# Statistics by positions, factors from PSUM, weights by quarters and differences by product in the opening of a hybrid decoder block

## The chip, the core and the metric

The kernel runs on one core of one Trainium2 chip. The metric is device microseconds for one execution, the median of several runs. TensorE (PE) multiplies 128x128 weights with 128x512 operands into PSUM, which has eight banks of 128x512 fp32; VectorE (DVE), ScalarE (ACT) and GpSimd (POOL) do the elementwise work, and SyncE (SP) issues all DMAs of this kernel, on one queue.

## The reference

One layer of a decoder block over 2048 positions of width 1024, in fp32. What matters here is its opening; the rest is named only.

```python
def rmsnorm(x, g):
    y = x * rsqrt(mean(x * x, axis=-1) + 1e-6)
    return y * g

h = rmsnorm(x, norm1_g)           # x: 2048 positions x 1024
proj = h @ w_in                   # 1024 x 3088
# split into q, k, v, g, a (gated linear attention) and b, c, h (short convolution)
# then: attention in chunks, convolution, output projection, residual,
# second rmsnorm, SwiGLU FFN of width 2816, residual, last rmsnorm
```

## The kernel before

**Layout.** Activations are kept with features on partitions and positions on the free axis. The 2048 positions are four blocks of 512 (`PB`), and a feature tile is 128 features; the input comes twice, as `xt` (features on partitions, 256 KB for one tile of one block) and as `x` (positions on partitions). Two blocks make a half; each stage runs for half 0 and then for half 1.

**Products.** Every fp32 matrix is split into a high part `hi` (ScalarE copies it to fp32r, L144) and a remainder `lo` (VectorE subtracts, L145), and a product is three matmuls: weight-hi with operand-hi, weight-hi with operand-lo, weight-lo with operand-hi. A unit (`unit`, matmuls at L321 to L323) does a 2x2 block product with seven products instead of eight (Winograd's form): weights A11, S1, S2, A12, S3, S4, A22 with operands B11, T1, T2, B21, T3, B22, T4. The T's are differences of the scaled input, made on GpSimd: T1 = B12 - B11, T2 = B22 - T1, T3 = B22 - B12, T4 = B21 - T2. The S's come from a 1 MB weight load `raw` of four quarters, also by GpSimd differences (L304 to L311).

**The opening**, which the change touches, is this. `first_stats` loads 16 tiles of `xt`, eight for block 0 and eight for block 1, with the first weights `raw` between them. ScalarE squares each tile (L418, L421), the squares of block 0 are added on VectorE and those of block 1 on GpSimd (L423), and a matmul with a matrix of ones sums over partitions (`column_rstd`, L159); `finish_rstd` makes the factor 1/sqrt(mean + eps), as a 128x512 tile in SBUF, with VectorE and ScalarE operations on the full tile (L165, then L149 to L153). `build_first` then goes through block 0 (`j` = 0) and block 1 (`j` = 1), and in each through eight feature tiles, called columns here: VectorE scales the tile with the norm's weight and factor (`scaled`, L431), ScalarE and VectorE split it into an operand `op` (L144, L145), and TensorE does six matmuls with it (L272 to L274), which give the first unit directly with the four quarters as they are. The VectorE instructions of a column are ordered so that the next tile's scaling stands ahead of the split of this one. The second block's `column_rstd` is issued within the first block (after column 3). After the 16 columns GpSimd makes the differences, column by column: for each of four `k` it does T1, T2, T3, T4 (L281), with one scratch tile `t1` for three of them, and each result is split.

**Order.** A scheduler orders the instructions of each engine by its own timeline; the order on an engine is then fixed, and an instruction waits for all ahead of it. `in_proj` runs twelve units for the half and, between the products of a unit, `tick` steps a queue of background work, in the order `gate_weights`, `gate` (the forget gate's matmuls L488 with `wa_sb`, and scans L516), `row_stats(2)`, `row_stats(3)`, and `h1_ahead`, which makes the operands of half 1.

**What exists already elsewhere.** `row_stats` makes the factors of blocks 2 and 3 from `x` by positions: ScalarE squares a piece with an accumulated sum (L388), VectorE and ScalarE make the factor on a 128x4 tile (L149 to L153), VectorE spreads each of its four columns over a 128x128 tile (L397), and TensorE transposes these into a PSUM bank `rb_ps` (L398), which ScalarE copies to SBUF.

Of the kernel before, what the change touches and what calls it, by code (L numbers as in the profile page):

```python
# [18 lines left out]
P = 128  # L19
D = 1024  # L20
SEQ = 2048
PB = 512
NB = SEQ // PB
KD = D // P
PT = PB // P
# [5 lines left out]
EPS = 1e-6  # L31
# [16 lines left out]
def tile_hymba_block(ctx, tc, x, xt, win, wa, wgu, wout, wffn, wdown, wdown_first, small, out):  # L48
# [7 lines left out]
    opp = pool_of("opp", 28)  # L56
# [139 lines left out]
    def split_op(src):  # L196
        o = opp.tile([P, 2, PB], F32R, name="op", tag="op")
        split(src, o[:, 0, :], o[:, 1, :])
        return o
# [45 lines left out]
            put("B22", k, b22)  # L245
            yield

    def build_first(quad, w, later):


        ops = {b: [] for _, b in PRODUCTS}
        h, o = {}, {}
        quarters = ("A11", "A12"), ("A21", "A22")
        los = []
        for j in range(2):
            for r in range(2):
                o[r, j] = bank()
            for k in range(KD):
                with ExitStack() as stack:
                    if len(los) > 1:  # L260
                        stack.enter_context(tc.issue_after(los[-2].ins))
                    h[k, j] = quad(k, j)
                x = opp.tile([P, 2, PB], F32R, name="op", tag="op")
                los.append(split(h[k, j][:], x[:, 0, :], x[:, 1, :]))
                if (j, k) == (0, 3):
                    rbs[1] = column_rstd(later, D)
                name = ("B11", "B12")[j] if k < 4 else ("B21", "B22")[j]
                ops.setdefault(name, []).append(x)
                c = slice(k % 4 * P, (k % 4 + 1) * P)
                for r in range(2):  # L270
                    q = w[quarters[r][k // 4]]
                    pe.matmul(o[r, j][:], q[:, 0, c], x[:, 0, :], start=k == 0, stop=False)  # L272
                    pe.matmul(o[r, j][:], q[:, 0, c], x[:, 1, :], start=False, stop=False)
                    pe.matmul(o[r, j][:], q[:, 1, c], x[:, 0, :], start=False, stop=k == KD - 1)  # L274
        for k in range(4):
            t1 = bt("t1")
            b11, b12, b21, b22 = h[k, 0], h[k, 1], h[k + 4, 0], h[k + 4, 1]
            for n, y, a, b in (
                ("T1", t1, b12, b11), ("T2", t1, b22, t1), ("T3", b12, b22, b12), ("T4", t1, b21, t1)
            ):  # L280
                pool.tensor_tensor(y[:], a[:], b[:], ALU.subtract)  # L281
                ops[n].append(split_op(y[:]))
        return ops, [(r, j, o[r, j], True) for j in range(2) for r in range(2)]

    def weight_quarter(src):
        n = src.shape[-1]
        h = wqp.tile([P, 2, PB], F32R, name="wq", tag="wq")[:, :, 0:n]
        split(src, h[:, 0, :], h[:, 1, :])
        return h

    def raw_weights(src):
        n = src.shape[-1]
        raw = rawp.tile([P, 4 * PB], F32, name="raw", tag="raw")[:, 0 : 4 * n]
        raw = raw.rearrange("p (a n) -> p a n", a=4)
        raw_loads.append(load(raw, src))
        return raw
# [79 lines left out]
        return s  # L376


    rbs = {}

    def row_stats(b):
        ssq = mtiny.tile([P, PT, 2], F32, name="ssq", tag="ssq")
        for t in range(PT):
            for e in range(2):
                xn = bt("xn")
                r0 = b * PB + t * P
                load(xn[:], x[r0 : r0 + P, e * PB : (e + 1) * PB])
                act.activation(xn[:], xn[:], AF.Square, accum_out=ssq[:, t, e : e + 1])  # L388
            yield
        v, l, y0 = [mtiny.tile([P, PT], F32, name=n, tag=n) for n in ("msq", "rl", "ry")]  # L390
        dve.tensor_tensor(v[:], ssq[:, :, 0], ssq[:, :, 1], ALU.add)
        dve.tensor_scalar(v[:], v[:], 1.0 / D, EPS, ALU.mult, ALU.add)
        rsqrt(v[:], v[:], l[:], y0[:])
        rb_ps = bank("rb_ps")
        for t in range(PT):
            rep = mtiny.tile([P, P], F32, name="rep", tag="rep")
            dve.tensor_copy(rep[:], v[:, t : t + 1].to_broadcast([P, P]))  # L397
            pe.transpose(rb_ps[:, t * P : (t + 1) * P], rep[:], ident[:])  # L398
        rb = bt("rb2")
        act.activation(rb[:], rb_ps[:], AF.Copy)  # L400
        store(s_rb[b][:], rb[:])

    raws, first_weights, last_load = {}, {}, []

    def first_stats():

        for j in range(2):
            for k in range(KD):
                h = bt("h") if j else tt("h")
                raws[j, k] = h  # L410
                last_load[:] = [load(h[:], xt[j, :, k, :])]
            if j == 0:
                raw = raw_weights(win[0])
        ssq = [tiny.tile([P, PB], F32, name="rb2", tag="rb") for _ in range(2)]
        for j in range(2):
            for k in range(KD):
                if k == 0:
                    act.activation(ssq[j][:], raws[j, k][:], AF.Square)  # L418
                else:
                    q = opp.tile([P, 2, PB], F32, name="q", tag="op")  # L420
                    act.activation(q[:, 0, :], raws[j, k][:], AF.Square)  # L421
                    add = pool if j else dve
                    add.tensor_tensor(ssq[j][:], ssq[j][:], q[:, 0, :], ALU.add)  # L423
            if j == 0:
                rbs[0] = column_rstd(ssq[0], D)
                for n, i in (("A11", 0), ("A21", 3), ("A12", 1), ("A22", 2)):
                    first_weights[n] = weight_quarter(raw[:, i, :])
        return ssq[1]

    def scaled(g, rb, h):  # L430
        dve.scalar_tensor_tensor(h[:], h[:], g, rb[:], ALU.mult, ALU.mult)  # L431
# [8 lines left out]
        split(raw[:], w[:, :, 0, :], w[:, :, 1, :])  # L440
        yield

    def build_h(later):


        def quad(k, j):
            return scaled(col(C_G1 + k), rbs[j], raws[j, k])

        return build_first(quad, first_weights, later)

    def h1_ahead():

# [486 lines left out]


    act.preload_act_table_set("natural_log_exp_and_others")
    later = first_stats()
    load(wgu_sb[:], wgu)
    ops, first = build_h(later)
    hurry.append(True)
    background.extend(
        [gate_weights(), gate(0, ops), row_stats(2), row_stats(3), unhurried(), h1_ahead()]
# [124 lines left out]
```

## Time and profile before

| | |
|---|---|
| median of 3 runs | 2182.29 us (2181.57 to 2185.2) |
| profiled execution | 2184.78 us |
| its span in the profile | 2183.0 us |
| granted TensorE clock, mean | 0.982 |
| busy: PE, DVE, ACT, POOL | 2048.8, 1460.2, 996.5, 985.5 us |
| moved by DMA | 467.65 MB |

The span runs from the first to the last instruction of the program; the profiled execution's time has 1.8 us around it. Busy is the time in which an engine executes; TensorE's is 94% of the span over the whole kernel, but not in the first 100 us, where the change is. Starts in the timeline are us from the span's beginning, and a row `x4` merges four instructions of one kind that follow each other; its second number is then the time from the start of the first to the end of the last. Instructions of one engine overlap at their ends, so the pace of a chain is the distance of starts, which is a little less than a duration. A name after `<-` in brackets is what ended the engine's wait.

### The profile page before, as it was taken

To read this page: it belongs to the slowest core of one execution; us is meant where nothing else is said; L and a number is where in the kernel's file an instruction comes from. 1 tells how busy PE (TensorE), PEld (TensorE's weight loads), DVE (VectorE), ACT (ScalarE), POOL (GpSimd) and SP (SyncE) were. 2 spreads that over 40 slices of the span, in tenths; PEclk is the share of its full clock that TensorE was granted. 3 is DMA by queue.
4 is the path that set the end of the run, shared out by engine and by line. 5 is a ranking of instruction groups with operands and counts; after the bars stand their busy time and mean duration, and the time that the engine had idled before them with its cause. 6 is when DMAs were issued, how large, how long until landed. Compare 5 with 4: busy or idle time off the path is not lost.

```text
span 2183.0 us, 26899 instructions
## 1 busy us (share of the span) xinstructions
PE 2048.8 (94%) x9137; PEld 1656.3 (76%) x9137; DVE 1460.2 (67%) x2039; ACT 996.5 (46%) x1940; POOL 985.5 (45%) x706
## 2 busy tenths in 40 slices
PE   4899899999998999999999989998999999989996
PEld 3577677877887887788888868887888888867774
DVE  7859975557763496787877566544666656668755
ACT  4555434564544245455555433333444544434442
POOL 4526431112201273555655456664544445357663
PEclk9999999999999999999999999999999999999998
DMA  4259667532586793466454595698353443598772
GB/s 147 71 202 321 215 246 258 150 111 91 156 289 198 295 309 138 164 234 223 174 227 174 214 357 209 245 347 348 116 183 135 159 160 134 221 361 315 304 266 101
DMA packets 189978, 467.65 MB, mean 214 GB/s; under 512 B 19856, under 2 KB 65168, under 8 KB 180112
## 3 DMA queue, kind: packets, MB, share of 16 engines
q1 hardware_dynamic: 189840, 465.93, 59.2%
q8 instruction: 72, 1.18, 0.2%
q14 instruction: 66, 0.54, 0.1%
HBM read 297.03 MB, written 168.82 MB: 213 GB/s over the span
## 4 chain that ended last, share of the span: by engine, by line
PE 68%; DVE 13%; DMA 9%; ACT 4%; issue 3%; POOL 2%; SPq 1%; DVEq 0%; ACTq 0%; POOLq 0%
PE mm L321 20%; PE mm L323 20%; PE mm L322 20%; DVE wq L145 2%; DVE h L431 2%; DMA op<-shT 1%; DVE op L145 1%; PE mm L709 1%; PE mm L710 1%; PE mm L712 1%; DMA op<-sm 1%; DMA op<-sa_T 1%; DVE c L345 1%; DMA raw<-in_wdown_first_dram 1%; DVE so L145 1%
## 5 line engine op out<-in xcount | busy, mean ns | idle before, releaser
L321 PE MATMUL mm<-op,wq 128*128 128x512 f32 x2495 | 984.2, 396 | 50.9 <-ACT c L341 22.2
L322 PE MATMUL mm<-op,wq 128*128 128x512 f32 x2495 | 977.9, 392 | 4.1 <-DVE op L145 4.1
L323 PE MATMUL mm<-op,wq 128*128 128x512 f32 x2495 | 967.2, 393 | 14.9 <-DVE wq L145 14.5
L145 DVE TENSOR_TENSOR wq<-raw,wq 128x512 fp32r<-128x512 f32 (+2 forms) x628 | 526.6, 845 | 337.8 <-ACT wq L144 335.6
L144 ACT ACTIVATE wq<-raw 128x512 fp32r<-128x512 f32 (+2 forms) x628 | 365.1, 587 | 580.2 <-PE mm L323 408.3
L321 PEld LDWEIGHTS mm<-op,wq 128*128 128x128 f32 x2495 | 471.7, 189 | 167.7 <-ACT c L341 30.7
L323 PEld LDWEIGHTS mm<-op,wq 128*128 128x128 f32 x2495 | 471.6, 189 | 124.7 <-DVE wq L145 24.4
L322 PEld LDWEIGHTS mm<-op,wq 128*128 128x128 f32 x2495 | 472.1, 189 | 102.9 <-DVE op L145 5.1
L306 POOL TENSOR_TENSOR raw<-s,raw 128x512 f32<-128x512 f32 (+2 forms) x98 | 131.5, 1342 | 461.5 <-DVE wq L145 427.2
L345 DVE TENSOR_TENSOR c<-mm,c 128x512 f32<-128x512 f32 x294 | 201.6, 686 | 102.6 <-PE mm L323 97.9
L304 POOL TENSOR_TENSOR s<-raw 128x512 f32<-128x512 f32 (+2 forms) x98 | 130.9, 1336 | 210.8 <-DMA raw<-in_wffn_dram 90.5
L341 ACT ACTIVATE c<-mm 128x512 f32<-128x512 f32 x294 | 170.7, 586 | 31.9 <-PE mm L323 30.8
L311 POOL TENSOR_TENSOR raw<-raw 128x512 f32<-128x512 f32 (+2 forms) x98 | 129.0, 1317 | 119.7 <-DVE wq L145 104.2
L865 POOL TENSOR_TENSOR y<-c,y 128x512 f32<-128x512 f32 x90 | 135.9, 1515 | 92.0 <-DVE c L345 91.8
L691 POOL TENSOR_TENSOR ssx<-ssx,q 128x512 f32<-128x512 f32 x52 | 75.9, 1472 | 144.1 <-ACT q L690 143.6
L305 POOL TENSOR_TENSOR raw<-raw 128x512 f32<-128x512 f32 (+2 forms) x98 | 137.2, 1400 | 4.7
L145 DVE TENSOR_TENSOR so<-t,so 128x512 fp32r<-128x512 f32 x100 | 88.0, 889 | 40.2 <-ACT so L144 39.9
L709 PE MATMUL mm<-op,wq 128*128 128x512 f32 x256 | 101.3, 396 | 0.0
L710 PE MATMUL mm<-op,wq 128*128 128x512 f32 x256 | 100.5, 393 | 0.0
L144 ACT ACTIVATE wq<-s 128x512 fp32r<-128x512 f32 (+2 forms) x98 | 57.5, 587 | 92.0 <-PE mm L323 87.6
L144 ACT ACTIVATE so<-t 128x512 fp32r<-128x512 f32 x100 | 62.7, 629 | 66.5 <-DMA sa_B<-so 35.3
L145 DVE TENSOR_TENSOR wq<-s,wq 128x512 fp32r<-128x512 f32 (+2 forms) x98 | 79.3, 810 | 14.8 <-ACT wq L144 14.2
(170 smaller groups left out, 1856.2 us busy)
## 6 DMA issues: line engine op xcount, KB each, us to landing
raw<-in_wffn_dram SPq DMA_DIRECT2D x44, 1024.0 KB, 5.6
sa_T<-so SPq DMA_DIRECT2D x88, 512.0 KB, 5.0
op<-sa_T SPq DMA_DIRECT2D x88, 512.0 KB, 8.4
sa_B<-so SPq DMA_DIRECT2D x69, 512.0 KB, 3.8
op<-sa_B SPq DMA_DIRECT2D x69, 512.0 KB, 8.6
raw<-in_win_dram SPq DMA_DIRECT2D x24, 1024.0 KB, 5.9
raw<-in_wdown_dram SPq DMA_DIRECT2D x24, 768.0 KB, 6.8
y<-sx SPq DMA_DIRECT2D x64, 256.0 KB, 6.7
```

What stands on the lines that cost most here:

```text
L144: last_hi[:] = [act.activation(hi, src, AF.Copy)]
L145: return dve.tensor_tensor(lo, src, hi.bitcast(F32), ALU.subtract)
L304: pool.tensor_tensor(s1, a21, a22, ALU.add)
L305: pool.tensor_tensor(a21, a11, a21, ALU.subtract)
L306: pool.tensor_tensor(a11, s1, a11, ALU.subtract)
L311: pool.tensor_tensor(a12, a12, a11, ALU.subtract)
L321: pe.matmul(o[:], wh, xh, start=first and k == 0, stop=False, skip_group_check=True)
L322: pe.matmul(o[:], wh, xl, start=False, stop=False, skip_group_check=True)
L323: return pe.matmul(o[:], wl, xh, start=False, stop=k == n - 1, skip_group_check=True)
L341: act.activation(t[:], o[:], AF.Copy)
L345: dve.tensor_tensor(t[:], o[:], t[:], ALU.add)
L865: eng.tensor_tensor(yy, c[:], yy, ALU.add)
```

## The change

1. **Statistics by positions.** The factors of blocks 0 and 1 are made as `row_stats` does it: `first_loads` loads four pieces of `x` for each block (128 positions x 1024, 512 KB each), ScalarE squares each with an accumulated sum (L411), and `rows_rstd` makes the factor on a 128x4 tile, spreads and transposes it. The 14 additions over tiles (L423), the two matmuls with ones and the full-size `finish_rstd` are gone from the opening. The squares of block 1 are issued within block 0's columns 4 to 7 (`row_squares`).
2. **Factors from PSUM.** `rows_rstd` returns the PSUM bank, and `scaled` reads it there (L437); `row_stats` still copies it to SBUF.
3. **Weights by quarters.** The first `raw` is loaded as four DMAs of 256 KB, two ahead of block 0's first four tiles of `xt` and two ahead of its last four. The order of loads is: four of `x`, two quarters, four tiles, two quarters, four tiles, four of `x` for block 1, eight tiles of block 1.
4. **Differences by product.** T1 is made for all four `k`, then T2, T3, T4, each in place in a tile of the scaled input (L283), without the scratch tile.

In the instruction lists as built, the change reaches to TensorE's row 416 of 8869, VectorE's 278 of 2041, ScalarE's 234, GpSimd's 58 and SyncE's 178; the rows after these are the same in both kernels. Within the lists of the changed kernel, GpSimd does T3 ahead of T2, and ScalarE has the splits of the two later weight quarters ahead of the split of the first operand. In the first block TensorE has the four transposes of block 1's factor behind the last matmul of block 0.

```diff
-    def build_first(quad, w, later):
+    def build_first(quad, w):
...
-                if (j, k) == (0, 3):
-                    rbs[1] = column_rstd(later, D)
+                if j == 0 and k >= PT:
+                    row_squares(1, k - PT)
...
-        for k in range(4):
-            t1 = bt("t1")
-            b11, b12, b21, b22 = h[k, 0], h[k, 1], h[k + 4, 0], h[k + 4, 1]
-            for n, y, a, b in (
-                ("T1", t1, b12, b11), ("T2", t1, b22, t1), ("T3", b12, b22, b12), ("T4", t1, b21, t1)
-            ):
-                pool.tensor_tensor(y[:], a[:], b[:], ALU.subtract)
-                ops[n].append(split_op(y[:]))
+            if j == 0:
+                rbs[1] = rows_rstd(squares[1])
+        for n, y, a, b in (
+            ("T1", (0, 0), (0, 1), (0, 0)), ("T2", (0, 0), (4, 1), (0, 0)),
+            ("T3", (0, 1), (4, 1), (0, 1)), ("T4", (0, 0), (4, 0), (0, 0)),
+        ):
+            for k in range(4):
+                yy, aa, bb = [h[k + dk, j] for dk, j in (y, a, b)]
+                pool.tensor_tensor(yy[:], aa[:], bb[:], ALU.subtract)
+                ops[n].append(split_op(yy[:]))
...
+    def rows_rstd(ssq):
+
         v, l, y0 = [mtiny.tile([P, PT], F32, name=n, tag=n) for n in ("msq", "rl", "ry")]
-        dve.tensor_tensor(v[:], ssq[:, :, 0], ssq[:, :, 1], ALU.add)
-        dve.tensor_scalar(v[:], v[:], 1.0 / D, EPS, ALU.mult, ALU.add)
+        dve.tensor_scalar(v[:], ssq[:, :, 0], 1.0 / D, EPS, ALU.mult, ALU.add)
         rsqrt(v[:], v[:], l[:], y0[:])
         rb_ps = bank("rb_ps")
         for t in range(PT):
             rep = mtiny.tile([P, P], F32, name="rep", tag="rep")
             dve.tensor_copy(rep[:], v[:, t : t + 1].to_broadcast([P, P]))
             pe.transpose(rb_ps[:, t * P : (t + 1) * P], rep[:], ident[:])
-        rb = bt("rb2")
-        act.activation(rb[:], rb_ps[:], AF.Copy)
-        store(s_rb[b][:], rb[:])
...
+        return rb_ps
+    def row_squares(b, t):
+        act.activation(rows[b, t], rows[b, t], AF.Square, accum_out=squares[b][:, t, 0:1])
+
+    def first_loads():
+
+        raw = rawp.tile([P, 4, PB], F32, name="raw", tag="raw")
+        for b in range(2):
+            squares[b] = mtiny.tile([P, PT, 2], F32, name="ssq", tag="ssq")
+            for t in range(PT):
+                xr = opp.tile([P, 2 * PB], F32, name="xr", tag="op")
+                rows[b, t] = xr[:]
+                r0 = b * PB + t * P
+                load(xr[:], x[r0 : r0 + P, :])
             for k in range(KD):
...
+                if b == 0 and k % 4 == 0:
+                    for i in ((0, 3), (1, 2))[k // 4]:
+                        raw_loads.append(load(raw[:, i, :], win[0][:, i, :]))
+                h = bt("h") if b else tt("h")
+                raws[b, k] = h
+                last_load[:] = [load(h[:], xt[b, :, k, :])]
+        for t in range(PT):
+            row_squares(0, t)
+        rbs[0] = rows_rstd(squares[0])
+        for n, i in (("A11", 0), ("A21", 3), ("A12", 1), ("A22", 2)):
+            first_weights[n] = weight_quarter(raw[:, i, :])
```

More of the change, by code (lines that the diff above doesn't have):

```diff
@@ L376, in silu @@
         return s
-    rbs = {}
     def row_stats(b):
@@ L398, in row_stats @@
             pe.transpose(rb_ps[:, t * P : (t + 1) * P], rep[:], ident[:])
-        rb = bt("rb2")
-        act.activation(rb[:], rb_ps[:], AF.Copy)
-        store(s_rb[b][:], rb[:])
-    raws, first_weights, last_load = {}, {}, []
-    def first_stats():
-        for j in range(2):
-            for k in range(KD):
[L409 to L428, printed above, removed]
@@ new lines, in rows_rstd @@
+        return rb_ps
+    rbs, raws, first_weights, last_load, rows, squares = {}, {}, {}, [], {}, {}
+    def row_squares(b, t):
[9 more added lines that the diff above has]
+                load(xr[:], x[r0 : r0 + P, :])
+            for k in range(KD):
+                if b == 0 and k % 4 == 0:
[9 more added lines that the diff above has]
+            first_weights[n] = weight_quarter(raw[:, i, :])
@@ L441, in gate_weights, with build_h @@
         yield
-    def build_h(later):
+    def build_h():
         def quad(k, j):
             return scaled(col(C_G1 + k), rbs[j], raws[j, k])
-        return build_first(quad, first_weights, later)
+        return build_first(quad, first_weights)
     def h1_ahead():
@@ L941, in tile_hymba_block @@
     act.preload_act_table_set("natural_log_exp_and_others")
-    later = first_stats()
+    first_loads()
     load(wgu_sb[:], wgu)
-    ops, first = build_h(later)
+    ops, first = build_h()
     hurry.append(True)
```

4 lines of the change are left out of this document (added).

## The prediction

> **What bounds the kernel now.** I read the page first, for its chain of waits, then the windows by stage, then the timeline of each engine up to 105 us.
>
> ```profile
> span 2183.0 us, 26899 instructions
> PE 68%; DVE 13%; DMA 9%; ACT 4%; issue 3%; POOL 2%; SPq 1%; DVEq 0%; ACTq 0%; POOLq 0%
> 24.38:44.01 19.63, 15.06 (x50) 10.63 (x50) 18.07 (x21) 6.92 (x11) 7.82 (x5) 1.00 0.00 0
> 44.01:63.78 19.77, 15.99 (x57) 11.07 (x57) 19.74 (x19) 7.84 (x13) 13.10 (x8) 0.91 0.08 28
> 63.78:101.34 37.56, 28.64 (x100) 19.41 (x99) 28.59 (x40) 19.15 (x38) 18.38 (x12) 0.86 0.17 59
> 101.34:160.00 58.66, 55.15 (x235) 43.95 (x234) 32.25 (x65) 33.62 (x80) 16.76 (x12) 0.97 0.60 202
> 160.00:250.00 90.00, 82.36 (x353) 64.96 (x352) 86.91 (x105) 45.82 (x81) 53.46 (x32) 1.00 0.84 285
> ```
>
> TensorE is 68% of the whole chain, but not in the opening. A window row has, after the length, busy time of PE, PEld, DVE, ACT, POOL, then the clock, the DMA share and GB/s. The first is block 0's columns: VectorE works 18.07 of 19.63 us. The second is block 1's: 19.74 of 19.77. In the third, where the differences are made and split, no engine is full (VectorE 28.59 of 37.56): that is a chain through several. Then TensorE is full (55.15 of 58.66), then VectorE (86.91 of 90). So up to 101 us time is set by VectorE and by what it waits for, and later work is a queue of full engines that starts when the opening hands over. As the instruction lists are the same from VectorE's row 278 of 2041 on, whatever the opening gains by its end stays, if nothing but the opening's results set its start.
>
> **Step 1: up to the first matmul.**
>
> ```profile
> 9.06 3.21 ACT L421 ACTIVATE q<-h 128x512 f32<-128x512 f32 x5 [2.14 <-DMA h<-in_xt_dram]
> 0.00:10.00 10.00, 0.00 (x0) 0.00 (x0) 3.16 (x9) 4.11 (x6) 1.11 (x7) 1.00 0.73 222
> 10.00:20.00 10.00, 2.08 (x2) 0.50 (x2) 7.44 (x10) 8.01 (x16) 2.42 (x2) 1.00 1.04 404
> 14.19 2.19 ACT L144 ACTIVATE wq<-raw 128x512 fp32r<-128x512 f32 x4 [1.91 <-DMA raw<-in_win_dram]
> 24.38 3.31 DVE L431 SCALAR_TENSOR_TENSOR h<-h,sml,rb 128x512 f32<-128x512 f32 x2
> 26.73 1.22 PE L272 MATMUL mm<-op,wq 128*128 128x512 f32 x2 [11.00 <-ACT op L144]
> 29.43 0.79 PE L273 MATMUL mm<-op,wq 128*128 128x512 f32 x1 [1.48 <-DVE op L145]
> 107.47 0.18 ACT L388 ACTIVATION_READ_ACCUMULATOR xn<-xn 128x1 f32 x1
> 117.33 0.21 ACT L149 ACTIVATE rl<-msq 128x4 f32<-128x4 f32 x1
> 118.50 0.15 DVE L152 SCALAR_TENSOR_TENSOR rl<-rl,msq 128x4 f32<-128x4 f32 x1
> 119.36 0.36 DVE L397 COPY rep<-msq 128x128 f32<-128x128 f32 x2
> L398 PE MATMUL rb_ps<-ident,rep x8: 272/273/273, 122.6 to 154.0; 128*128 128x128 f32 x8
> ```
>
> Before, 2 MB of `xt` are squared by 9.06 + 3.21 = 12.27, and the first scaling starts at 24.38. The 12.1 us between are the additions' tail, the matmul with ones and the full-size factor, much of it beside GpSimd's additions. After, the same 2 MB come as pieces of `x`. The last square before started at 9.06 + 3.21 - 0.64 = 11.6, so I take the last piece there. It has twice the columns, so at most 2 x 0.64 us, and 0.18 for the sum: 13.1. The small chain, priced by `row_stats`: mean 0.2, one weight split that stands ahead on ScalarE 0.5, Ln 0.21, another split 0.5, Exp 0.21, three small VectorE operations of 0.15 (0.6 more for a split between), two copies 0.36, transposes 0.27, two copies, transposes, with handovers of 0.1: 4 us. The first scaling is at 17, 7.4 us earlier.
>
> The first split must also wait, on ScalarE, behind the two later weight quarters. Before, 3.15 MB had landed at 14.19; those quarters end at 4.19 MB, and at 404 GB/s the other 1.04 MB take 2.6 us: 16.8. With 0.5 for its split, the first operand's high part and matmul are at 18.2, against 26.73. VectorE does two scalings (1.3 us) and two weight splits (1.2) ahead of the first `lo`, so the first matmul on it starts at about 20.1, against 29.43: **9.3 us earlier**. Bounds: if the pieces of `x` land at 404 GB/s from the start, up to 3 us more; if the 2.09 MB after 11.6 come at the 222 GB/s of the first 10 us, 4.19 MB land at 21 and it is 4 us less.
>
> **Step 2: block 0.**
>
> ```profile
> 35.20 0.74 DVE L431 SCALAR_TENSOR_TENSOR h<-h,sml,rb 128x512 f32<-128x512 f32 x1
> 35.86 0.68 DVE L145 TENSOR_TENSOR op<-h,op 128x512 fp32r<-128x512 f32 x1
> 36.46 0.74 DVE L431 SCALAR_TENSOR_TENSOR h<-h,sml,rb 128x512 f32<-128x512 f32 x1
> 30.45 0.63 PE L273 MATMUL mm<-op,wq 128*128 128x512 f32 x1
> 30.88 0.63 PE L274 MATMUL mm<-op,wq 128*128 128x512 f32 x1
> 43.33 0.39 PE L274 MATMUL mm<-op,wq 128*128 128x512 f32 x1
> 44.01 1.42 DVE L431 SCALAR_TENSOR_TENSOR h<-h,sml,rb 128x512 f32<-128x512 f32 x2
> DMA packets 3024, 7.49 MB, mean 187 GB/s; under 512 B 464, under 2 KB 592, under 8 KB 2640
> ```
>
> A column costs VectorE 0.66 + 0.60 when GpSimd is still: eight columns from 17.0 with the weight splits end by 29. TensorE is behind: its first matmuls are 0.43 us apart, while later 235 take 55.15 (0.235 each). Before, it went from 29.43 to 43.7; after, with 12 of 48 at 0.43 and 36 at 0.235, 13.6 us: 33.7. The four squares of block 1 add 4 x 1.4 us to ScalarE, whose eight splits are 4.2: 9.8 us, inside that. They wait for loads: 7.34 MB must land, at 404 GB/s at 24.6; the splits of columns 6 and 7 stand behind the last square, so VectorE ends at 29, still ahead of TensorE. In all 11.8 MB are loaded instead of 7.49, by 35.6; the second weights, which GpSimd needs third, land at 33.
>
> **Step 3: between the blocks.** Before, the second factor is made under block 0, and block 1 starts at 44.01. After, the small chain and two copies lie under TensorE's tail, but the transposes stand behind its last matmul: two transposes, two copies, two transposes, about 1 us. Block 1's first scaling is at 34.6, **9.4 us earlier**. Without that cover (TensorE done first) the whole 4 us chain would show.
>
> **Step 4: block 1, with GpSimd.**
>
> ```profile
> 69.57 3.44 DVE L145 TENSOR_TENSOR wq<-raw,wq 128x512 fp32r<-128x512 f32 x2
> 69.06 1.72 POOL L281 TENSOR_TENSOR t<-h,t 128x512 f32<-128x512 f32 x1
> L431 DVE SCALAR_TENSOR_TENSOR h<-h,sml,rb x48: 736/1185/1783, 24.4 to 799.2; 128x512 f32<-128x512 f32 x48
> L345 DVE TENSOR_TENSOR c<-mm,c x294: 656/691/694, 86.1 to 2138.4; 128x512 f32<-128x512 f32 x147
> L734 DVE TENSOR_TENSOR y<-y,mm x32: 669/678/690, 660.4 to 833.8; 128x512 f32<-128x512 f32 x32
> L670 DVE SCALAR_TENSOR_TENSOR osb<-ot,sml,gt x16: 741/746/751, 327.1 to 711.0; 128x512 f32<-128x512 f32 x16
> 63.78 0.68 DVE L145 TENSOR_TENSOR op<-t,op 128x512 fp32r<-128x512 f32 x1
> ```
>
> Where GpSimd is busy, a VectorE instruction with both inputs in SBUF goes at 1.68 us instead of 0.60 (two in 3.44, less the overlap), and scalings reach 1.78. Those with one input in PSUM never do: 294 of L345 between 0.656 and 0.694, 16 scalings of L670 at most 0.751. So the new scaling should cost 0.66 to 0.75 whatever GpSimd does, and hide under it. GpSimd now has T1 to make from the first scaling on and doesn't pause, so each `lo` of block 1 takes 1.68. Two scalings 1.3, eight `lo` 13.4, two weight splits of the second unit 3.4, that of `wa` 1.4: 19.5, so 54.1, against 63.78 before, where the same took 19.8. **9.7 us earlier**. Bounds: no contention, 46; scalings that contend after all, 8 x 1.0 more, 62.
>
> The Trainium skill ("SBUF — State Buffer", Who interferes with whom) has the pair of ports as an exclusive lock that is held for a whole instruction, and a VectorE instruction with at most one SBUF input free of it. The second half is what L345 shows. By the first half a turn would be a whole GpSimd instruction and a whole split, about 0.2 us more than the 1.68 of the rows and some 4 us more over steps 4 and 5 (an estimate from that page); the rows decide, and I keep 1.68.
>
> **Step 5: the differences.**
>
> ```profile
> 101.34 0.69 DVE L145 TENSOR_TENSOR wq<-raw,wq 128x512 fp32r<-128x512 f32 x1
> L145 DVE TENSOR_TENSOR op<-t,op 128x512 fp32r<-128x512 f32 x12 | 9.5, 806 | 8.1 <-ACT op L144 8.1
> L281 POOL TENSOR_TENSOR t<-h,t 128x512 f32<-128x512 f32 x8 | 12.2, 1520 | 18.4 <-DVE op L145 18.4
> 83.84 1.30 POOL L281 TENSOR_TENSOR t<-h,t 128x512 f32<-128x512 f32 x1 [3.96 <-DVE op L145]
> 105.16 0.62 PE L323 MATMUL mm<-op,wq 128*128 128x512 f32 x2
> ```
>
> From 63.78 to the first weight split of the second unit, at 101.34, VectorE is busy 28.59 us and idle 9.0, of which 8.1 wait for ScalarE's split of a difference, while GpSimd waits 18.4 us for VectorE: T2 must wait until T1 has been split, as both use `t1`, and so on four deep. By product there are four independent columns between T1 and T2 of one `k`, so these waits mostly go; I keep 3 of 9 us (bounds 0 and 9), for the gate's own chain. VectorE's list has three instructions fewer here (1.9 us), and meets 11 GpSimd instructions, nearly all contended, instead of about 7 (12 at a mean of 1.53, between 1.30 for one that met nothing and 1.72): 4 x 1.07 = 4.3 more. So 28.6 - 1.9 + 4.3 + 3 = 34.0: the second unit's first split is at 88.1, **13.2 us earlier**.
>
> TensorE before used that split only at 105.16, 3.2 us after it was done, as twelve matmuls of the first unit stood ahead; after, it can use it at once, so TensorE may be up to 16.5 us ahead. The next splits come from VectorE, so I take a third of the way from 13.2: **14.3 us**.
>
> **Step 6: the rest.** From here on TensorE (55.15 of 58.66) and VectorE (86.91 of 90) set the time before, and would equally after. Lists differ in places up to VectorE's row 278, about 257 us; I price that at nothing, with 2 us either way. The sum against the profiled execution: 2184.8 - 14.3 = 2170.5; against the median, which is 2.5 us below it, 2182.3 - 14.3 = **2168.0 us**.
>
> **The rivals.**
>
> (a) *Differences gain nothing* (12%): GpSimd and VectorE, in turns at 1.68 us, take in step 5 as long as the waits did. Then only 9.7 remain: 2172.6. For it: GpSimd is the busier here; against: 18.4 us of its idle time were waits for one scratch tile.
>
> (b) *The loads land sooner* (13%): pieces of 4 KB rows at 404 GB/s from the start, 3 us more: 2165. For it is the rate from 10 us on; against, the slow start, which may be no matter of row length.
>
> (c) *The scalings contend after all* (6%), so that the change doesn't do what it says: step 4 ends at 62, and 6 us remain at the most: 2176; with (a), 2180, which can't be told from no change. Against it are all 342 rows with a PSUM input.
>
> (d) *Slower: TensorE stays at half clock* (6%). In the opening it would work in short bursts at VectorE's pace (3 matmuls in 1.7 to 3.4 us); before, the clock from 63.78 to 101.34 was 0.86. At 0.43 instead of 0.235 a matmul costs 0.195 more. It decides from 96 matmuls on (14.3 + 4.4 us), all of them where TensorE is the bound, after 88; if the 235 of the fourth stage all ran so, it would be 45.8 us more: 2214. Against it: TensorE has steady work in the fourth stage, and was granted 0.97 there.
>
> The Trainium skill ("TensorE: Matmul & The Clock Gate", What's actually happening) has the clock halve after an idle window of about 3.4 us and return after about as long busy. By it (d) could not last once step 6 is reached, and the 0.97 agrees.
>
> **How the numbers follow.** About 58% go to the steps as summed, whose own errors (3 us in step 1, 3 in step 5, 2 in step 6) give 2162 to 2174. With (a), (b) and most of (c), the range is 2160 to 2177; (d), a gain lost altogether (5%) and the tails stay out. A measurement here can tell 0.2%, 4.4 us. Faster by more than that: 0.58 + 0.12 + 0.13 + 0.05 = 0.88; within it, 0.06; slower, 0.06.
>
> **What would show it.** Right: the first L437 near 17 us, first matmul of a column near 18; all 16 L437 under 0.8 us; block 1's first scaling near 34.6 behind the transposes; `lo` splits of block 1 at 1.7 us; VectorE's waits for a difference's split near nothing; the first L325 of the second unit near 89. Wrong: L437 at 1.7, GpSimd's or VectorE's idle time back between 54 and 88, a clock under 0.9 after 90, or a stage from 100 to 250 us that is longer than before.

## The result, and the profile after

The changed kernel takes 2174.31 us (median of 14 runs, 2166.73 to 2178.24), the kernel before beside it 2183.92 us (14 runs, 2176.81 to 2187.82). The ratio is 0.9952, 95% interval 0.9939 to 0.9965, so by the ratio 10.5 us less (7.6 to 13.3). In a second series it was 2171.85 us against 2184.18: 0.9936, interval 0.9923 to 0.9949. Faster was right, and the time lies in the range of 2160 to 2177; the forecast of 14.3 us less is a little more than the first interval holds, and inside the second.

The profiled execution was the fastest of the 14 runs, which matters below. First the page: its span and the chain that ended last.

```profile
span 2165.0 us, 26920 instructions
PE 66%; DVE 13%; DMA 9%; POOL 3%; issue 3%; ACT 3%; SPq 1%; DVEq 0%; POOLq 0%; ACTq 0%
```

The chain looks as before: the changed stages are a small share of it. What moved is seen in the windows, cut at the same events as before: block 0's columns from the first matmul on a `lo`, block 1 from its first scaling, the differences up to the second unit's first weight split, the stretch up to half 1's first scaling, and the one from there to half 1's last split.

```profile
18.40:31.54 13.14, 12.89 (x51) 10.22 (x50) 9.58 (x21) 8.41 (x17) 0.00 (x0) 1.00 1.04 402
31.54:50.90 19.36, 17.03 (x61) 11.98 (x62) 19.32 (x19) 9.39 (x17) 18.01 (x11) 0.91 0.18 72
50.90:82.62 31.72, 25.72 (x91) 18.00 (x90) 31.69 (x38) 16.90 (x33) 18.54 (x11) 0.89 0.19 66
82.62:139.00 56.38, 54.54 (x237) 42.79 (x236) 30.89 (x63) 32.82 (x80) 17.14 (x12) 1.00 0.59 197
139.00:227.17 88.17, 77.97 (x328) 61.24 (x327) 82.16 (x93) 43.96 (x77) 50.47 (x31) 0.98 0.83 284
```

Block 0 is now TensorE's (12.89 of 13.14 us), block 1 VectorE's as before (19.32 of 19.36), and where the differences are made VectorE, which was idle for 9 of 37.56 us, is full: 31.69 of 31.72. Then comes what the prediction had not looked into: the row of 88.17 us, VectorE busy for 82.16 of them. Before, the same work took less:

```profile
101.34:156.59 55.25, 51.74 (x220) 41.13 (x219) 28.84 (x61) 31.50 (x77) 15.02 (x11) 0.97 0.59 201
156.59:242.14 85.55, 79.44 (x343) 63.20 (x342) 82.46 (x95) 45.20 (x79) 52.86 (x32) 1.00 0.86 293
```

So the lead over before is 18.7 us at the second unit's split (82.62 against 101.34), 17.6 at half 1's first scaling (139.00 against 156.59), and 15.0 at its last split (227.17 against 242.14).

The timeline of the opening, engine by engine, in order of time:

```profile
15.04 1.41 DVE L437 SCALAR_TENSOR_TENSOR h<-h,sml,rb_ps 128x512 f32<-128x512 f32 x2 [0.57 <-PE rb_ps L405]
15.49 1.32 ACT L144 ACTIVATE wq<-raw 128x512 fp32r<-128x512 f32 x2 [3.45 <-DMA raw<-in_win_dram]
18.40 0.70 PE L273 MATMUL mm<-op,wq 128*128 128x512 f32 x1
21.03 0.63 PE L273 MATMUL mm<-op,wq 128*128 128x512 f32 x1
21.46 0.53 PE L274 MATMUL mm<-op,wq 128*128 128x512 f32 x1
21.82 0.39 PE L273 MATMUL mm<-op,wq 128*128 128x512 f32 x1
22.05 0.39 PE L274 MATMUL mm<-op,wq 128*128 128x512 f32 x1
30.45 0.38 PE L405 MATMUL rb_ps<-ident,rep 128*128 128x128 f32 x2
31.04 0.47 PE L405 MATMUL rb_ps<-ident,rep 128*128 128x128 f32 x2 [0.21 <-DVE rep L404]
31.54 1.41 DVE L437 SCALAR_TENSOR_TENSOR h<-h,sml,rb_ps 128x512 f32<-128x512 f32 x2 [0.42 <-PE rb_ps L405]
57.24 3.43 DVE L145 TENSOR_TENSOR op<-h,op 128x512 fp32r<-128x512 f32 x2
60.59 3.43 DVE L145 TENSOR_TENSOR wq<-raw,wq 128x512 fp32r<-128x512 f32 x2
```

The first scaling waits for the transposes, the first matmul for the later weight quarters; TensorE's starts are 0.43 us apart until 21.8 and 0.23 after that; the transposes stand behind block 0's last matmul; and where GpSimd is busy two splits take 3.35 us from start to start (57.24 to 60.59), 1.68 each. The group of the new scaling, from the answer for its line (shortest, median and longest in ns):

```profile
L437 DVE SCALAR_TENSOR_TENSOR h<-h,sml,rb_ps x16: 733/741/747, 15.0 to 44.1; 128x512 f32<-128x512 f32 x16
```

### The profile page after: what moved, and what is told of

Read it like the earlier page. It is cut to its first block, busy times and chain, and to the rows that moved or that the text cites. A ratio compares the mean times of both kernels' runs of the same rounds, so it can differ in the third digit from the quotient of the medians.

```text
span 2165.0 us, 26920 instructions
## 1 busy us (share of the span) xinstructions
PE 2048.1 (95%) x9141; PEld 1658.2 (77%) x9141; DVE 1447.6 (67%) x2040; ACT 993.1 (46%) x1940; POOL 977.1 (45%) x699
## 4 chain that ended last, share of the span: by engine, by line
PE 66%; DVE 13%; DMA 9%; POOL 3%; issue 3%; ACT 3%; SPq 1%; DVEq 0%; POOLq 0%; ACTq 0%
PE mm L323 20%; PE mm L325 19%; PE mm L324 19%; DVE wq L145 3%; DVE op L145 2%; DMA op<-shT 2%; DVE h L437 2%; PE mm L715 1%; PE mm L716 1%; PE mm L718 1%; DVE so L145 1%; DMA op<-sm 1%; DVE c L347 1%; POOL ssx L697 1%; DVE lo L145 1%
## 5 line engine op out<-in xcount | busy, mean ns | idle before, releaser
L323 PE MATMUL mm<-op,wq 128*128 128x512 f32 x2495 | 985.4, 397 | 44.5 <-ACT wq L144 18.7
L145 DVE TENSOR_TENSOR wq<-s,wq 128x512 fp32r<-128x512 f32 (+2 forms) x98 | 79.7, 814 | 14.3 <-ACT wq L144 13.7
```

Of the source, the lines that this page charges most:

```text
L145: return dve.tensor_tensor(lo, src, hi.bitcast(F32), ALU.subtract)
L323: pe.matmul(o[:], wh, xh, start=first and k == 0, stop=False, skip_group_check=True)
```

## The experiments

The question was where the gain went: 18 us between the two profiles, 9.6 between the medians, and which of the four parts it comes from. Ratios are to the kernel before, run on the same chip; 0.1% is 2.2 us.

| kernel | median us (runs) | ratio | 95% interval |
|---|---|---|---|
| before again | 2182.64 (10) | 0.9996 | 0.9983 to 1.0008 |
| changed, again | 2171.85 (6) | 0.9936 | 0.9923 to 0.9949 |
| without part 2 | 2177.45 (12) | 0.9972 | 0.9962 to 0.9982 |
| without part 4 | 2171.71 (5) | 0.9943 | 0.9931 to 0.9956 |
| without part 3 | 2169.62 (6) | 0.9933 | 0.9914 to 0.9951 |
| before with part 4 alone | 2187.62 (12) | 1.0010 | 0.9998 to 1.0022 |
| factors kept | 2160.04 (5) | 0.9886 | 0.9869 to 0.9902 |
| factors kept, without part 4 | 2167.21 (6) | 0.9917 | 0.9901 to 0.9934 |
| pieces of `x` in half rows | 2170.07 (5) | 0.9943 | 0.9923 to 0.9963 |
| factors kept, without part 3 | 2159.83 (5) | 0.9890 | 0.9871 to 0.9909 |
| opening reordered | 2170.86 (6) | 0.9938 | 0.9919 to 0.9956 |
| opening reordered, factors kept | 2165.86 (5) | 0.9910 | 0.9887 to 0.9932 |

**The same kernels again: how much is chance.** No edit.

> The kernel before, unchanged, for a second profile. Theory M (the opening always hands over at the same time, and executions differ afterwards by stretches of 3.4 us in which TensorE is granted half its clock): counted from the end of VectorE's list, the rows between 390 and 615 us stand within 1 us of those of the first profile of this kernel; half-clock stretches after 100 us may be more or fewer, and the span follows their number. Rival R (the opening itself varies from execution to execution, with its loads): those rows stand 3 us or more away from the first profile's.

> The changed kernel, unchanged, for a second profile. Its first profile was its fastest execution (2166.73 us against a median of 2174.3). Theory M: the rows between 390 and 615 us stand within 1 us of those of its first profile, so 14.5 us earlier than before, and a longer span shows as more half-clock stretches of 3.4 us after 100 us. Rival R: the handover is only some 10 us earlier, as the first profile had early loads by chance; then the first scaling or the first difference stands 3 us or more later than in the first profile.

Counted from the end of VectorE's list, the second profile of before stands within 0.2 us of the first from 389 to 545 us (0.6 us at one place, near 400), as theory M has it. From there to 620 us it is 1.7 us later, more than the 1 us that M allowed but by the cause that M names: the second has a stretch of 3.4 us at half clock from 539.8, where the first was granted 1.00. The second profile of the changed kernel is neither theory's. Its last piece of `x` is squared at 9.70 instead of 9.29, its first scaling is at 16.36 instead of 15.04, and it runs 1.1 us behind the first from then on to the second unit's split. The spans of the changed kernel's two profiles, 2165.0 and 2171.6, differ by 6.6: 1.1 us comes from the opening, and the rest builds up later, along with TensorE's clock.

```profile
core 0: 2165.0 us, clock 0.983
core 0: 2171.6 us, clock 0.979
```

The first is the first profile, the second the second one. A difference of 0.004, which is rounded, over 2168 us is some 9 us of clock. In the record it is stretches of 3.4 us at half clock: the second profile has five that the first has not, and the first one that the second has not. Here are two windows of the second profile, and then the two of the first at the same work (times less 1.6 and 2.3 us, by which VectorE's rows differ there):

```profile
224.00:227.40 3.40, 2.96 (x8) 1.85 (x7) 3.40 (x4) 0.63 (x1) 2.23 (x2) 0.50 0.68 205
527.80:531.20 3.40, 3.40 (x13) 2.98 (x12) 3.40 (x10) 1.59 (x5) 0.00 (x0) 0.50 0.42 135
```

```profile
222.40:225.80 3.40, 1.85 (x9) 1.22 (x8) 3.40 (x4) 0.63 (x1) 2.27 (x2) 1.00 0.74 235
525.50:528.90 3.40, 3.40 (x20) 2.93 (x19) 3.40 (x10) 1.17 (x4) 0.00 (x0) 1.00 0.41 135
```

The column before the last two is the clock: 0.50 against 1.00, and in the second window 13 matmuls against 20. The 14 runs of the first series show the same spread: the four below 2171.5 us have clocks of 0.980 to 0.984, the four above 2175 of 0.979 or 0.980. So the pair of profiles with 18 us between them compares a lucky execution with an ordinary one. Against before, the second profile is 13.4 us ahead at half 1's last split and 11.6 at the end. That is the ordinary case, and the medians (9.6 and 12.3 less) say the same.

**Part 2 undone: the factor copied to SBUF.**

```diff
-                rbs[1] = rows_rstd(squares[1])
+                rbs[1] = in_sbuf(rows_rstd(squares[1]))
...
+    def in_sbuf(rb_ps):
+        rb = tiny.tile([P, PB], F32, name="rb2", tag="rb")
+        act.activation(rb[:], rb_ps[:], AF.Copy)
+        return rb
...
-        rbs[0] = rows_rstd(squares[0])
+        rbs[0] = in_sbuf(rows_rstd(squares[0]))
```

> Undoes the second part alone: ScalarE copies the factor from PSUM to SBUF and the scalings read it there. My theory (a scaling with one input in PSUM is not slowed by GpSimd): the scalings of block 1 go from 0.74 to 1.7 us while GpSimd is busy, so block 1 ends up to 8 us later; GpSimd is then further ahead with its differences, so the first weight split of the second unit is 4 to 8 us later, and the whole time 4 to 7 us longer than the changed kernel's. Rival (the reading from PSUM changes nothing): scalings stay at 0.74, less than 1 us later at the handover (the copies of 0.5 us alone).

From its timeline of VectorE, a scaling, a split and a scaling in block 1:

```profile
47.86 1.77 DVE L442 SCALAR_TENSOR_TENSOR h<-h,sml,rb 128x512 f32<-128x512 f32 x1
49.55 0.68 DVE L145 TENSOR_TENSOR op<-h,op 128x512 fp32r<-128x512 f32 x1
50.16 1.77 DVE L442 SCALAR_TENSOR_TENSOR h<-h,sml,rb 128x512 f32<-128x512 f32 x1
```

Six of block 1's eight scalings take 1.76 or 1.77 us instead of 0.74. The split after each takes only 0.68 instead of 1.12, as GpSimd, which waits for the scaled tile, is idle just then (0.7 us ahead of each of its differences): a column has a pitch of 2.30 us against 1.70, not 1 us more. Block 1's last scaling is 4.9 us later (50.16 against 45.22 in the changed kernel's second profile), the second unit's split 4.4 (88.15 against 83.71) and the whole 5.6 by the medians, with intervals that do not touch (beside the changed kernel's first series, 0.9939 to 0.9965, they overlap by a little). The reading from PSUM is worth what it was expected to be, and what it gains is kept.

**Part 4 undone: differences by column; and part 4 alone.** The edits put the old loop back, and put the new loop into the kernel before.

> Undoes the fourth part alone: the differences are made column by column again, with one scratch tile. My theory (step 5): block 1 ends as in the changed kernel or a little sooner (GpSimd meets fewer splits), then VectorE waits 6 to 8 us for splits of differences again and GpSimd some 15 us for VectorE; the first weight split of the second unit is 3 to 6 us later than in the changed kernel (82.6), the whole time 3 to 6 us longer. Rival (a) of the prediction (turns of GpSimd and VectorE take as long as the waits did): the split stands within 1 us, and the whole time is the same.

> The kernel before with the fourth part alone: differences by product. Prediction's step 5: the first weight split of the second unit is some 4 to 6 us earlier than before (101.3), and the time 4 to 5 us shorter. After the run by column (which was as fast as the changed kernel) I now hold the other view: the split is earlier by 4 us or so, but VectorE and TensorE lose that again between 100 and 200 us, in waits for loads and for the gate's work, and the whole time is within 2 us of before's.

By column the second unit's split is at 86.49, 3.9 us later than in the changed kernel's first profile, whose block 1 starts at almost the same time (31.54 against 31.74): step 5 of the prediction, as expected. But the whole time is the same, and not 3 to 6 us longer. Part 4 alone has that split at 92.91, 8.4 us earlier than before and twice what was expected, and the time is not shorter at all. The windows show where this is lost: by column, then part 4 alone; in each, up to half 1's first scaling and on to its last split.

```profile
140.66:225.65 84.99, 79.35 (x343) 63.24 (x342) 82.15 (x95) 45.17 (x79) 53.50 (x32) 1.00 0.86 295
```

```profile
92.91:158.00 65.09, 60.89 (x255) 47.04 (x254) 37.81 (x73) 34.12 (x84) 15.92 (x12) 0.97 0.53 188
158.00:247.12 89.12, 79.29 (x333) 62.46 (x331) 82.87 (x94) 44.63 (x77) 51.07 (x31) 0.98 0.81 277
```

With part 4 alone half 1's first scaling is at 158.00, no earlier than before (156.59), although the split was 8.4 us earlier. This is what stands ahead of it: SyncE issues the first tiles of `xt` for it at 151.76, behind four stores of `sv` that began at 139.34 (before: at 150.82), and on VectorE there is a split of weights that waits 2.11 us for ScalarE. And from there to the last split it takes 89.12 us instead of 85.55. By column, in the changed kernel, that stretch takes 84.99; by product 88.17. VectorE's work there is the same (82.15 and 82.16), so the 3.2 us are waits. This is what VectorE waited for in the changed kernel (us in total, times, longest; the wait of 2.1 us is ahead of the first scaling), then SyncE and the two scalings with the longest waits, and how a third wait, 1.31 us at 148.15, came about, from the chain that ended last:

```profile
DVE h L437 <- DMA h<-in_xt_dram: 4.4, 4, 2.1
DVE h L437 <- DMA rb<-srb: 3.0, 1, 3.0
```

```profile
123.95 11.42 SPq L139 DMA_DIRECT2D sv<-c  x4
135.42 1.40 SPq L136 DMA_DIRECT2D h<-in_xt_dram  x3
139.00 0.75 DVE L437 SCALAR_TENSOR_TENSOR h<-h,sml,rb 128x512 f32<-128x512 f32 x1 [2.14 <-DMA h<-in_xt_dram]
145.42 1.41 DVE L437 SCALAR_TENSOR_TENSOR h<-h,sml,rb 128x512 f32<-128x512 f32 x2 [3.04 <-DMA rb<-srb]
```

```profile
136.54 0.50 ACT rb L393
137.06 4.94 DMA srb<-rb
142.02 0.32 SPq L136
...
144.05 4.07 DMA h<-in_xt_dram
148.15 0.06 DVE h L437
```

Half 1's first scaling waits for a tile of `xt` that SyncE issues at 135.42, behind four stores of `sv`, the results of a unit. The factor of block 3 is made at 136.54, stored to DRAM, and may be loaded back only when the store has landed, 4.94 us later, so the next scaling waits for it until 145.42; behind that load on SyncE's queue stands the next tile of `xt`. By column the store took 2.06 us, with only one tile of `xt` near it and that issued behind it, at 139.41:

```profile
139.04 0.33 SPq L139 DMA_DIRECT2D srb<-rb  x1
141.10 0.33 SPq L136 DMA_DIRECT2D rb<-srb  x1
```

**The factors kept in SBUF.** If that round trip is where the lead goes, taking it away should bring it back.

```diff
-        rb = bt("rb2")
-        act.activation(rb[:], rows_rstd(ssq)[:], AF.Copy)
-        store(s_rb[b][:], rb[:])
+        rbs[b] = tiny.tile([P, PB], F32, name="rb2", tag="rb")
+        act.activation(rbs[b][:], rows_rstd(ssq)[:], AF.Copy)
...
-        rb = []
-        for j in range(2):
-            r = tiny.tile([P, PB], F32, name="rb2", tag="rb")
-            load(r[:], s_rb[2 + j][:])
-            rb.append(r)
+        rb = [rbs[2], rbs[3]]
```

> The changed kernel, but the factors of blocks 2 and 3 stay in SBUF, without the store to DRAM and the load back. Theory L: the lead of 4 us that differences by product gives TensorE (20.3 us earlier than before at 139 to 148 us of the changed kernel, against 15.9 by column) is lost at 139 to 155 us, where VectorE waits 2.1, 3.0 and 1.3 us for two tiles of xt and for the factor of block 3, which SP issues late, behind stores. Without the factor's round trip some 3 us of it stay: 2 to 4 us shorter than the changed kernel (2171.9). Rival: VectorE's own work from 140 to 200 us sets the time, as it is full there, and it is within 1 us.

> Both: differences by column, and the factors of blocks 2 and 3 kept in SBUF. Theory L: by column VectorE waited only 0.8 us for that factor, so this gains at most 1 us over the run by column (2171.7), and by product is then worth 2 to 3 us. Rival (VectorE's work sets the time): the same as by product with the factor kept.

Kept and by product: 2160.04 us, 11.8 less than the changed kernel, about three times the upper end of what was expected. Kept and by column: 2167.21, 4.5 less than by column, where at most 1 was expected. From the two timelines' windows, by product first:

```profile
82.00:115.94 33.94, 33.94 (x147) 26.74 (x146) 23.87 (x55) 24.34 (x66) 11.08 (x8) 1.00 0.76 266
115.94:204.51 88.57, 83.28 (x354) 67.74 (x353) 78.13 (x87) 48.22 (x84) 51.20 (x32) 0.96 0.82 286
```

```profile
117.89:206.24 88.35, 81.97 (x356) 65.44 (x355) 78.48 (x87) 46.99 (x82) 51.10 (x32) 1.00 0.81 286
```

```profile
115.94 0.74 DVE L437 SCALAR_TENSOR_TENSOR h<-h,sml,rb 128x512 f32<-128x512 f32 x1
```

The last row is by product again: half 1's first scaling starts at 115.94 without a wait, 23 us earlier than in the changed kernel, and the stretch from there is no shorter (88.57). So the gain is the earlier start, and the 4.94 us of the store cannot be all of it: the changed kernel's first scaling, at 139.00, did not wait for that factor at all. What differs more is the order of the lists. Here SyncE issues the first tiles of `xt` at 99.87, ahead of stores of `sv`, and not at 135.42 behind four of them, and ScalarE copies the factor of block 3 at 123.70 and not at 136.43. TensorE is full from 82 to there (33.94 of 33.94): of the 22.7 us at the last split (204.51 against 227.17), 8.3 are left at 320 us. There by product is 5.2 us ahead of by column (23.3 against 18.2 ahead of before), of which 0.9 were there at block 1's first scaling already (32.40 against 33.26), and 7.2 by the medians, though the two intervals just meet. So with the factors kept, the lead that part 4 makes seems to reach the end.

One thing stays open. Without the round trip the schedule puts half 1's work earlier in the lists, from about 100 to 270 us. No run has that order together with the store, or the old order without it, so how much of the 11.8 us belongs to each is not shown.

**Part 3 undone: one load of 1 MB.**

```diff
-                if b == 0 and k % 4 == 0:
-                    for i in ((0, 3), (1, 2))[k // 4]:
-                        raw_loads.append(load(raw[:, i, :], win[0][:, i, :]))
...
+            if b == 0:
+                raw_loads.append(load(raw[:], win[0]))
```

> Undoes the third part alone: the first weights come in one load of 1 MB, behind the eight tiles of block 0, instead of by quarters. My theory (step 1): the weights land some 4 us later than the first quarters did (19 instead of 15), so the first matmul is 3 to 4 us later, and, as TensorE sets the end of block 0, block 1's first scaling is 2 to 4 us later; the whole time is 2 to 4 us longer than the changed kernel's. Rival: the scalings of block 0 go ahead meanwhile and TensorE catches up at full clock, less than 1 us.

> The changed kernel with the factors of blocks 2 and 3 kept in SBUF (2160.0 in its first run), and without the third part: one load of 1 MB for the first weights. TensorE's list is the same as with quarters. If the quarters are worth what the first study of them showed (block 1 starts 2.5 us later without them, 1.3 us of it left at the second unit), the time is 1 to 2 us longer than with quarters; if the later stages hide it, the same.

The first matmul is at 19.07 (17.38 by quarters in the first profile, 18.11 in the second), 1.0 to 1.7 us later and not 3 to 4, block 1's first scaling at 34.00 (31.54 and 32.66), the second unit's split at 83.96 (82.62 and 83.71). So 1.3 to 2.5 us at block 1 become 0.3 to 1.3 at the split, and nothing at the end: 2169.62 against 2171.85, and with the factors kept 2159.83 against 2160.04. By quarters the first scaling waits for more ahead of it (15.04 against 13.78, two weight splits stand in the small chain), which gives part of it back.

**The rate of the first loads.** Each piece of `x` comes in two loads of 512 columns; the lists of the compute engines are the same.

```diff
-                load(xr[:], x[r0 : r0 + P, :])
+                for e in range(2): load(xr[:, e * PB : (e + 1) * PB], x[r0 : r0 + P, e * PB : (e + 1) * PB])
```

> The changed kernel, but each of the eight pieces of x comes in two loads of 512 columns (rows of 2 KB in place of 4 KB); the order of instructions on the compute engines is the same. Rival (b) of the prediction, row length sets the early rate: the first 2 MB land 2 to 3 us later than in the changed kernel (11.6 instead of 9.0, as the tiles of xt did before), the first scaling is at 17 to 18 instead of 15.0, and the time is 1 to 3 us longer. Other view, the order of the loads or the issue sets it: they land within 0.7 us of 9.0, apart from the four more issues of 0.45 each on SyncE.

The row of its last square, and that of the changed kernel in its first and second profile:

```profile
10.92 1.06 ACT L411 ACTIVATE xr<-xr 128x1024 f32<-128x1024 f32 x1
```

```profile
9.29 1.06 ACT L411 ACTIVATE xr<-xr 128x1024 f32<-128x1024 f32 x1
```

```profile
9.70 1.06 ACT L411 ACTIVATE xr<-xr 128x1024 f32<-128x1024 f32 x1
```

Halves are 1.2 to 1.6 us later and so a little over half of the way to the 11.6 of before, where SyncE's eight issues took as long (3.73 us, against 3.74 here and 1.84 for four). Row length and number of issues change together here, and are not told apart, and the result lies between the two views. The first scaling is at 16.29, no later than in the second profile, block 1's is at 33.99, 1.3 us later than there, and the time is the same.

**A faster opening, tried.** The four copies of the factor go to one tile, block 1's squares stand one column earlier (columns 3 to 6; the expectation says two), its factor is made ahead of block 0's last column, and the two later weight quarters are split at column 2 instead of ahead of the first operand.

```diff
+                if (j, k) == (0, 2):
+                    for n, i in (("A12", 1), ("A22", 2)):
+                        w[n] = weight_quarter(first_raw[0][:, i, :])
+                if (j, k) == (0, KD - 1):
+                    rbs[1] = rows_rstd(squares[1], opp.tile([P, PT, P], F32, name="reps", tag="op"))
...
-                if j == 0 and k >= PT:
-                    row_squares(1, k - PT)
+                if j == 0 and 2 < k < KD - 1:
+                    row_squares(1, k - 3)
...
```

> Tried for a faster opening: the changed kernel with the four copies of the factor in one tile (no copy waits for a transpose), the squares of block 1 two columns earlier, and its factor made before the last column of block 0. Block 1's first scaling 0.5 to 2 us earlier (31.5 in the changed kernel), and as much of it at the end as the later stages leave: 0 to 2 us shorter than 2171.9.

> Both: that opening, and the factors of blocks 2 and 3 kept in SBUF. If TensorE's queue hands on what the opening gains, 0.5 to 2 us shorter than with the factors kept alone (2160.0); if VectorE's work from 116 to 205 us and the order there set the end, the same.

Block 1's first scaling is at 31.39, against 31.54 and 32.66 in the changed kernel, and with the factors kept at 30.48 against 32.40. So it is 0.2 to 1.9 us earlier, and the times are not clearly shorter: 2170.86 against 2171.85, and with the factors kept 2165.86 against 2160.04, longer but with intervals that overlap. The version to keep is the changed kernel with the factors in SBUF: 1.14% less than before (0.98 to 1.31).

## Why the prediction was right, point by point

**Step 1** (first scaling at 17, first `lo` matmul at 20.1): 15.04 and 18.40, and 16.36 and 19.63 in the second profile, so 11.0 or 9.8 us earlier instead of 9.3. The mis-sized term is the loads: the last piece of `x` was taken at 11.6 as that of `xt` before, and came at 9.29 and 9.70. Rival (b) had this direction, and half rows show that the kind of load has a part in it. The small chain took 4.6 us (10.44 to 15.04) instead of 4; its terms alone add up to 3.9, before the handovers.

**Step 2** (TensorE ends block 0 at 33.7): 30.45. The slow start was right (0.43 us until 21.8, then 0.23; ten such matmuls for the twelve assumed). Of the 3.2 us, 1.7 are the earlier start. The rest is a matter of size: from the first `lo` on, two of the 48 matmuls and two of the slow ones were already done, and the fast ones were 0.227 us apart and not 0.235.

**Step 3** (block 1 from 34.6): 31.54, by the same 3 us. The chain lay under TensorE's tail, and the transposes stood behind it, as said.

**Step 4** (new scaling 0.66 to 0.75, block 1 19.5 us): 0.733 to 0.747 for all 16, and 19.36 us. Undoing it put the scalings at 1.77, so rival (c) falls. A column's scaling and split together had the pitch of 1.70 us that was assumed for the split alone, with the scaling hidden. The Trainium skill ("SBUF — State Buffer", Who interferes with whom) is borne out where it frees an instruction with one input outside SBUF: no scaling was slowed. For its lock of a whole instruction the prediction had worked out turns some 0.2 us longer than 1.68; the turns after the scalings are 1.68 (57.24 to 60.59).

**Step 5** (34.0 us, the split at 88.1, 13.2 earlier): 31.7 us, the split at 82.62, 18.7 earlier. VectorE's idle time went altogether, where I kept 3 us for the gate's own chain. Part 4 measured alone gives 8.4 us at this place. So rival (a), that turns at 1.7 us eat the gain, falls as a mechanism.

**Step 6** (the rest keeps it) is the step that failed, and the one that hid the errors of the others. Of the 18.7 us, 15.0 reached half 1's last split in the first profile, and 13.4 in the second. A sign that the prediction had named for being wrong is there as well, a stage between 100 and 250 us that is longer than before: 56.38 against 55.25, and 88.17 against 85.55. The prediction argued from two full engines, and one of its rows, VectorE busy for 86.91 of 90 us, was true. But what VectorE does there is half 1's work, and that does not start when the second unit starts: the first scaling (139.00) waited 2.14 us for a tile of `xt` that stood on SyncE's queue behind stores of the units' results, and the next (145.42) 3.04 us for the factor of block 3 on its way through DRAM. I had priced the queue behind the handover at nothing and did not follow SyncE's queue into it.

So rival (a)'s conclusion held in the end: of the total, part 4 is worth nothing (2171.71 without it), and the 10 to 12 us of the medians come from the opening up to block 1's end, 12.9 us earlier in the first profile and 11.8 in the second, where the sum had 9.7. Of these, part 2 has 5.6 and part 3 nothing that can be measured; the rest would be part 1's, the statistics by positions, if the parts add up, but it was not run alone. That the total fits is in part luck: the sum had 2 to 3 us too little for the opening, and 4.6 us for step 5 and its handover of which nothing is left at the end.

**Rival (d)**, TensorE at half clock: the clock from 82.62 to 139.00 was 1.00. The Trainium skill ("TensorE: Matmul & The Clock Gate", What's actually happening), by which it could not last, agrees with that; and the stretches of half clock that the profiles show later are 3.4 us or small multiples of it, the window it names, but for one of about 18 to 21 us at the very end. What the prediction lacked is that such stretches come and go from one execution to the next, and move the time by several microseconds.

## What to carry to other kernels

A lead counts only up to the next event that does not depend on it: follow it to what starts the next full stretch (here tiles and a factor that come through one shared queue, behind other work), not only to the next full engine. If a part gives no time alone, try it again with the next bound taken away: by product was worth nothing with the round trip, and 4 to 7 us without it, though two intervals that just meet leave that a little unsure. One pair of profiles can be a lucky one; compare their clocks before a difference of half a per cent is explained.

## What was not expected of the hardware

A store of 256 KB issued right behind three loads of the same size took 4.94 us until what waited for it could go on, and 2.06 us where they were not just ahead of it. The five other profiles with the same order have 4.25 to 5.17 us until it landed, and three more without it 2.00 to 2.23. Stretches of 3.4 us at half clock lie at the same work in one execution and not in the next (0.50 against 1.00 in the same stage), and the means of 0.979 and 0.983 go with spans of 2171.6 and 2165.0. Where GpSimd waits for the tile that VectorE scales, only one VectorE instruction in two is slowed (1.77, then 0.68), so the loss from a factor in SBUF was 0.6 us a column, not 1.
